# Other order at the stage borders of a Strassen-style macaron block, and the mixer's weight tiles at high addresses

## The chip, the cores and the metric

The kernel runs on one core of a Trainium2 chip. The metric is the device time of one execution in microseconds (us). The engines are TensorE (PE in the profile, with its weight loads as PEld), VectorE (DVE), ScalarE (ACT) and GpSimd (POOL); SyncE (SP) issues most transfers. Each engine works through its own queue in a fixed order and waits at an instruction until what it needs is there.

## The reference

One layer on x of 1024 tokens by 1024 channels, all in float32:

```
x = x + 0.5 * SwiGLU_1(RMSNorm(x))          # FFN 1: gate, up 1024x2816, down 2816x1024
h = RMSNorm(x); p = h @ W_in                # u, v of the gating; q, k, v, z, b, a of the delta rule
x = x + concat(A, B) @ W_out                # A: chunked spatial gating, B: gated delta rule, 4 heads of 128
x = x + 0.5 * SwiGLU_2(RMSNorm(x))          # FFN 2, the same sizes
y = RMSNorm(x)
```

`swiglu(x) = (silu(x @ w_gate) * (x @ w_up)) @ w_down`. In B the short convolution, SiLU and an L2 norm are put on the queries and keys, and a decay matrix `exp(g_i - g_j)` per head and chunk is made from the a column group of the projection.

## The kernel before

**Products.** Each float32 operand is split into a high and a low part (`split`, L60 to L62: ACT casts the high part, DVE subtracts it to get the low part), and `mm3` (L53) makes three matmuls of one product: high by high, high by low, low by high. The FFNs are computed with seven products instead of eight. `Combos` (L107) holds the transposed, normed x as quarters B11, B12, B21, B22 and as four combinations T1 to T4 of them. For 128 tokens at a time, `blocks` transposes (L95, TensorE with an identity) two token tiles, and writes the quarters and the combinations with `put` (ACT L118 high part, then DVE or POOL L119 low part).

**FFN.** `ffn` (L173) loads the gate and up weights of 22 column blocks (`load_gu`, L189, tiles `graw`, POOL makes the combinations `s` at L199, and the split tiles are `ga` and `gs`). Block 0 is done with plain products (`gu_plain`, L237) in two halves of 256 columns each, so that it can begin when half of x is normed; blocks 1 to 21 use the seven products (`gu`, L257), which need all of B and T. `start1` (L475) and `start2` (L625) hold the order of this beginning: norms of x (ACT square, DVE scale at L82 or L502), `blocks`, the two `gu_plain`. Between blocks, sums of weights and hidden values are stored for the down products. The down stage (L367 to L444) works through 7 rows of a plan (k = 0 to 6) with 6 units each, a unit being a left and a right tile that are loaded (`prepare`, L377, three units ahead), split (tile `unit`) and multiplied.

**FFN 1 to mixer.** While the last rows of the down stage run, each finished token tile is normed and transposed into `hT` (`to_mid`, L518). `z0` (L528) is a filler handed to `ffn`: its weights (`zraw`, split to `wz`) are loaded first, and it then makes 8 token tiles' first half of z and of the b and a columns. It allocates in the pools of FFN 1 (`sf`, `graw`). `middle` (L684) follows: the a columns become `xa` (L745 to L762), a matmul with `csa` (L763 to L766) sums them along the chunk, the result goes out and comes back broadcast as `grb`, and `decay` (L780) makes the decay matrices E from that (DVE L791 to L796, ACT exponentials). `v0` is the first half of the values, 8 token tiles of 24 matmuls; `keys` (L879) makes the keys of a head with the convolution (`pad`, `acc`, L863 to L869) and their transposes (`kst`, L838).

**Mixer to FFN 2.** The last of the mixer are the u1 products (mm<-wk at L53). Then 16 groups of transposes bring the mixer's output into `yT` (ACT and DVE `actT`), and `w_out` (L577) multiplies by W_out, whose weight tiles `wo` are split in the `gsp` ring of FFN 2.

**What sets the order.** The program is written as Python generators. A list scheduler of the tile framework puts each engine's queue in order from the order in which the code is written and from when tiles come free. Tiles live in pools; the pools of a stage are laid one behind the other in SBUF in the order in which they are opened, and those of the next stage lie over them, so a new tile waits for the old tile at its address. Opened at L555 to L561 are the mixer's pools: in the program before, its weight tiles `wk` (pool `wp`) lie at byte 114112 to 146880 of a partition, over FFN 1's `graw` and `sf` and what lies next to them, and FFN 2's `wo` tiles at 181184 to 209856 lie over the key tiles `kst` and their neighbours..

## Time and profile before

| | before |
|---|---|
| median of 3 runs (lowest to highest) | 1855.46 us (1854.37 to 1859.35) |
| profiled execution: time / span in the profile | 1855.36 us / 1853.6 us |
| mean granted TensorE clock | 0.988 |
| busy: PE, DVE, ACT, POOL | 96%, 63%, 37%, 40% |

In the rows of a timeline, the columns are start, busy time, engine, line, operation, out<-in, tile size, how many are put together, and in brackets the idle time of that engine just before and who released it. A table of windows gives for each stretch the engines' busy time with their number of instructions, and then PEclk, the granted clock (1.00 is full).

### The profile page before, as it was taken

Reading aid. Unit: us, or ns where it says so; the run is one execution under the profiler, and the core shown is the slowest. Engines: PE = TensorE matmul, PEld = TensorE weight load, DVE = VectorE, ACT = ScalarE, POOL = GpSimd, SP = SyncE. Lnnn points to the kernel's source line nnn. Section 1 sums busy time; section 2 is a strip of 40 time slices with the busy share of each in tenths; the row PEclk is TensorE's granted clock in tenths of the full one; section 3 lists DMA queues with packets and bytes.
Section 4 is the critical chain, followed back from the end, with each engine's and each line's share of the span. In section 5 each row is a group of like instructions: output and inputs, shape, how many; then the busy total and the mean of one; then the engine's idle time right before and its main releaser. Section 6 shows DMA issues by size and latency. Waiting matters only on the chain.

```text
span 1853.6 us, 25526 instructions
## 1 busy us (share of the span) xinstructions
PE 1788.0 (96%) x9735; PEld 1529.8 (83%) x9735; DVE 1175.8 (63%) x1529; ACT 685.8 (37%) x1193; POOL 746.7 (40%) x585
## 2 busy tenths in 40 slices
PE   5999999998999998998999999989999999999997
PEld 4888888887788888998788999978888888878886
DVE  6867776554565474668755344587676776656546
ACT  5433333322443353432344542443333323244433
POOL 5567576564140012121032420366576665614001
PEclk8999999999999998999999999999999999999999
DMA  5254444534957444454432354334544445495744
GB/s 206 102 171 140 165 139 150 185 138 168 337 190 261 135 168 138 139 178 131 145 87 71 92 199 138 114 97 148 176 148 161 152 141 177 152 337 193 263 144 148
DMA packets 134732, 302.27 MB, mean 163 GB/s; under 512 B 27441, under 2 KB 42065, under 8 KB 134609
## 3 DMA queue, kind: packets, MB, share of 16 engines
q1 hardware_dynamic: 132112, 296.20, 47.2%
q10 hardware_dynamic: 2496, 4.44, 0.7%
q8 instruction: 76, 1.25, 0.3%
q14 instruction: 48, 0.39, 0.1%
HBM read 208.83 MB, written 91.77 MB: 162 GB/s over the span
## 4 chain that ended last, share of the span: by engine, by line
PE 82%; DVE 6%; DMA 4%; POOL 3%; issue 2%; ACT 1%; SPq 0%; POOLq 0%; DVEq 0%; ACTq 0%
PE mm L53 46%; PE ax L53 33%; PE ax L95 1%; POOL s L199 1%; PE sd L53 1%; DMA graw<-in_f2gu_dram 1%; POOL rs L70 1%; DVE acc L867 1%; POOL t L286 1%; PE sc L53 1%; DMA left<-hq 1%; DVE E L791 0%; POOL s L286 0%; DVE unit L62 0%; DVE o L82 0%
## 5 line engine op out<-in xcount | busy, mean ns | idle before, releaser
L53 PE MATMUL mm<-unit 128*128 128x512 f32 x1056 | 243.1, 390 | 5.7 <-ACT unit L61 3.9
L199 POOL TENSOR_TENSOR s<-graw 128x512 f32<-128x512 f32 x84 | 129.2, 1538 | 273.8 <-DMA graw<-in_f2gu_dram 128.5
L53 PEld LDWEIGHTS mm<-unit 128*128 128x128 f32 x1056 | 197.6, 188 | 48.3 <-ACT unit L61 4.7
L62 DVE TENSOR_TENSOR ga<-graw,ga 128x512 fp32r<-128x512 f32 x134 | 152.0, 1136 | 108.6 <-ACT ga L61 107.9
L61 ACT CAST gs<-s 128x512 fp32r<-128x512 f32 x168 | 104.1, 622 | 297.6 <-PE ax L53 144.6
L62 DVE TENSOR_TENSOR unit<-left,unit 128x1024 fp32r<-128x1024 f32 x84 | 101.8, 1215 | 137.2 <-ACT unit L61 137.2
L53 PE MATMUL ax<-T,gs 128*128 128x512 f32 x792 | 183.1, 389 | 0.0
L53 PE MATMUL ax<-unit 128*128 128x512 f32 x792 | 180.5, 389 | 0.0
L53 PEld LDWEIGHTS ax<-T,gs 128*128 128x128 f32 x792 | 148.7, 188 | 30.9
L53 PEld LDWEIGHTS ax<-unit 128*128 128x128 f32 x792 | 148.7, 188 | 30.9
L62 DVE TENSOR_TENSOR gs<-s,gs 128x512 fp32r<-128x512 f32 x168 | 169.3, 1009 | 2.5 <-ACT gs L61 0.3
L61 ACT CAST unit<-left 128x1024 fp32r<-128x1024 f32 x84 | 82.5, 982 | 235.9 <-PE ax L53 101.8
L53 PE MATMUL mm<-B,ga 128*128 128x512 f32 (+1 forms) x864 | 167.1, 348 | 0.2 <-DVE ga L62 0.2
L53 PE MATMUL mm<-T,gs 128*128 128x512 f32 x720 | 166.4, 389 | 0.0
L53 PEld LDWEIGHTS mm<-T,gs 128*128 128x128 f32 x720 | 135.1, 188 | 28.1
L53 PEld LDWEIGHTS mm<-B,ga 128*128 128x128 f32 x864 | 140.3, 195 | 19.2 <-DVE ga L62 0.4
L53 PE MATMUL mm<-actT,wk 128*128 128x512 f32 x576 | 150.2, 402 | 0.0
L70 POOL TENSOR_TENSOR rs<-rs,half 128x1 f32<-128x1 f32 (+1 forms) x29 | 20.2, 697 | 317.5 <-DVE rs L76 317.4
L53 PE MATMUL mm<-wk,actT 128*128 128x256 f32 x960 | 126.5, 289 | 2.3 <-ACT wk L61 1.8
L53 PE MATMUL ax<-B,ga 128*128 128x512 f32 x528 | 127.1, 390 | 0.0
L53 PEld LDWEIGHTS mm<-wk,actT 128*128 128x128 f32 x960 | 120.2, 195 | 3.5 <-ACT wk L61 2.1
L53 PEld LDWEIGHTS mm<-actT,wk 128*128 128x128 f32 x576 | 103.5, 188 | 19.1 <-ACT ev L736 0.2
(239 smaller groups left out, 3044.4 us busy)
## 6 DMA issues: line engine op xcount, KB each, us to landing
left<-hq SPq DMA_DIRECT2D x70, 512.0 KB, 5.0
graw<-in_f1gu_dram SPq DMA_DIRECT2D x44, 512.0 KB, 5.5
wq<-t SPq DMA_DIRECT2D x44, 512.0 KB, 2.8
hq<-s SPq DMA_DIRECT2D x44, 512.0 KB, 3.2
graw<-in_f2gu_dram SPq DMA_DIRECT2D x44, 512.0 KB, 5.0
right<-wq SPq DMA_DIRECT2D x40, 512.0 KB, 4.9
wd<-in_f1wd_dram SPq DMA_DIRECT2D x22, 512.0 KB, 6.6
hq<-sg SPq DMA_DIRECT2D x22, 512.0 KB, 3.7
```

What stands on the lines that cost most here:

```text
L53: nc.tensor.matmul(*args, **kw)
L61: nc.scalar.copy(h, src)
L62: nc.vector.tensor_tensor(l, src, h, op=ALU.subtract)
L70: nc.gpsimd.tensor_tensor(o, i, half[:, :w], op=ALU.pow)
L95: nc.tensor.transpose(ps[:, i * P:(i + 1) * P], blk(i), ident)
L199: nc.gpsimd.tensor_tensor(f, u, v, op=op)
L286: nc.gpsimd.tensor_tensor(o, u, v, op=op)
L867: nc.vector.scalar_tensor_tensor(acc, pad[:, j:j + 512], cw[:, blk, j:j + 1], acc, op0=ALU.mult, op1=ALU.add)
```

## The change

The order at the borders between the stages is written differently, and some tiles move. No arithmetic is changed.

- **Beginning of the FFNs.** `put_sums` takes the splits of T1 to T4 out of `blocks`; all of them come after the second `gu_plain`. The norms of the second half of x are written ahead of the first `gu_plain`. The sums of the second half are held in the x pool. x is loaded in the order 0, 4, 1, 5 and 2, 6, 3, 7, the second four earlier.
- **Down stage.** `prepare` loads the right tile first.
- **z.** The weights are loaded as two tiles of 1088 columns in the ring `post`, which the down stage's right tiles use too, and z's products go to the banks "mm" instead of "ax".
- **Mixer.** The pools are opened in another order: `wk` now lies at byte 176576 to 211392, above all others, and its tiles have 2176 columns. The weights of v0 are loaded ahead of the rest of `middle`, and three of v0's token tiles come before the sum along the chunk.

```diff
...
 
-        def sums(self):
-            return [self.qp.tile([P, 2, 512], F32, tag="post", name="f", bufs=4) for _ in range(2)]
-
-
-        def blocks(self, i, pp, xns, uv, b12=None, late=False, eng=nc.gpsimd):
+        def sums(self, p=None):
+            if p is None:
+                return [self.qp.tile([P, 2, 512], F32, tag="post", name="f", bufs=4) for _ in range(2)]
+            return [p.tile([P, 2, 512], F32, tag="x", name="f") for _ in range(2)]
+
+
+        def blocks(self, i, pp, xns, uv, b12=None):
             def tr(j, q):
...
             nc.vector.tensor_tensor(t2, b22p, t1, op=ALU.subtract)
+            self.put("B22", i, b22p, nc.vector)
             nc.vector.tensor_tensor(t4, b21p, t2, op=ALU.subtract)
-            self.put("B22", i, b22p, nc.vector)
-            yield
-            if not late:
-                self.put("T2", i, t2, nc.vector)
+            yield
+
+        def put_sums(self, i, names, engs):
+            t3, t1, t2, t4 = self.f[i]
+            for n, eng in zip(names, engs):
+                if n == "T3":
+                    nc.gpsimd.tensor_tensor(t3, t2, t3, op=ALU.subtract)
+                self.put(n, i, {"T1": t1, "T2": t2, "T3": t3, "T4": t4}[n], eng)
                 yield
-            self.put("T1", i, t1, nc.gpsimd)
-            yield
-            nc.gpsimd.tensor_tensor(t3, t2, t3, op=ALU.subtract)
-            self.put("T3", i, t3, eng)
-            yield
-            if not late:
-                self.put("T4", i, t4, eng)
-                yield
-
-        def late(self, i):
-            _, _, t2, t4 = self.f[i]
-            self.put("T2", i, t2, nc.vector)
-            yield
-            self.put("T4", i, t4, nc.gpsimd)
-            yield
 
...
             left, right = gtile(F32, "left"), post("right")
-            nc.sync.dma_start(left[:, :n], hq[u][:, l, :n])
             if isinstance(r, tuple):
...
                 nc.sync.dma_start(right[:, :n], wq[u][:, r, :n])
+            nc.sync.dma_start(left[:, :n], hq[u][:, l, :n])
             t = bp.tile([P, 2, 2, 2, 512], F32R, tag="cmb", name="unit", bufs=3)
...
     nc.scalar.dma_start(ident, a["cst"][:, 0:P])
-    xs = load_x(xdram, (0, 1))
+    xs = load_x(xdram, (0, 4))
     g = grow("ffn1_norm")
-    xs.update(load_x(xdram, (4, 5)))
+    xs.update(load_x(xdram, (1, 5)))
 
...
             next(weights)
+            xs.update(load_x(xdram, (2, 6, 3, 7)))
             b = b12()
...
             together(*parts, n=2)
-            together(*parts, weights, n=2)
-            xs.update(load_x(xdram, (2, 3, 6, 7)))
-            f.gu_plain(slice(0, 256), b)
+            together(*parts, weights)
             rest = xi(2) + xi(3)
...
                 nc.vector.scalar_tensor_tensor(x, x, rs[:, i:i + 1], g, op0=ALU.mult, op1=ALU.mult)
-            together(*parts)
+            f.gu_plain(slice(0, 256), b)
             b = b12()
-            parts = [cb.blocks(i, f.X, xi(i), cb.sums(), b, eng=nc.vector) for i in range(2, 4)]
-            together(*parts, n=4)
+            for i in range(2, 4):
+                together(cb.blocks(i, f.X, xi(i), cb.sums(xp), b))
             f.gu_plain(slice(256, 512), b)
-            together(*parts)
+            V, G = nc.vector, nc.gpsimd
+            together(*(cb.put_sums(i, ("T2", "T1", "T3", "T4"), (V, G, V, G)) for i in range(4)))
 
...
             for i in range(4):
-                r = rp.tile([P, 544], F32, tag="sf", name="zraw", bufs=4)
-                nc.sync.dma_start(r, a["wz0"][i // 2][:, i % 2 * 544:i % 2 * 544 + 544])
+                if i % 2 == 0:
+                    raw = qp.tile([P, 1088], F32, tag="post", name="zraw", bufs=4)
+                    nc.sync.dma_start(raw, a["wz0"][i // 2])
+                r = raw[:, i % 2 * 544:i % 2 * 544 + 544]
                 w = rp.tile([P, 2, 544], F32R, tag="graw", name="wz", bufs=4)
...
             for t in range(8):
-                o = bank(ps[1], "ax")
+                o = bank(ps[0], "mm")
                 h = st["hT"][t // 4]
...
         ps_a, ps_s, ps_m = psums(mid, (2, 1, 3))
-        wp = pool(mid, "wp")
+        tl = pool(mid, "tl")
+        up = pool(mid, "up")
+        lv = pool(mid, "lv")
         ep = pool(mid, "ep")
         ts = pool(mid, "ts")
-        up = pool(mid, "up")
-        tl = pool(mid, "tl")
-        lv = pool(mid, "lv")
         kp = pool(mid, "kp")
+        wp = pool(mid, "wp")
         yblk = middle(tc, nc, a, locals())
...
                 normed(x, g2, x, junk)
-            together(cb.blocks(i, pp, xi, uv, b, late=True))
+            together(cb.blocks(i, pp, xi, uv, b))
+            together(cb.put_sums(i, ("T1", "T3"), (nc.gpsimd, nc.gpsimd)))
         together(second)
...
             together(f.load_gu(0, True))
-            f.gu_plain(slice(0, 256), b)
             xns = {}
...
                     normed(xs[i + 4 * j], g2, xns[i][j])
+            f.gu_plain(slice(0, 256), b)
             c = b12()
-            parts = [cb.blocks(2, pp, xns[2], cb.sums(), c)]
-            together(*parts, n=4)
-            together(cb.late(0), cb.late(1))
-            parts.append(cb.blocks(3, pp, xns[3], cb.sums(), c))
-            together(parts[1], n=4)
+            for i in range(2, 4):
+                together(cb.blocks(i, pp, xns[i], cb.sums(xp), c))
             f.gu_plain(slice(256, 512), c)
-            together(*parts)
+            V, G = nc.vector, nc.gpsimd
+            together(*(cb.put_sums(i, ("T2", "T4"), (V, G)) for i in range(2)),
+                     *(cb.put_sums(i, ("T2", "T1", "T3", "T4"), (V, G, V, G)) for i in range(2, 4)))
 
...
 
-    def load_w(src):
+
+    def load_w(src, off=0):
         raw = wp.tile([P, src.shape[-1]], F32, tag="raw", name="raw", bufs=2)
         nc.sync.dma_start(raw, src)
-        s = wp.tile([P, 2, src.shape[-1]], F32R, tag="wk", name="wk", bufs=4)
+        s = wp.tile([P, 2176], F32R, tag="wk", name="wk", bufs=4)[:, off:off + 2048].rearrange("p (s n) -> p s n", s=2)
         split(s[:, 0], s[:, 1], raw)
...
 
-    def token_steps(srcs, n, evac, act, tiles=range(8), part=KC):
-        ws = [load_w(s).rearrange("p s (k n) -> p s k n", k=4) for s in srcs]
+    def token_steps(srcs, n, evac, act, tiles=range(8), part=KC, ahead=False):
+        ws = [load_w(s, 16).rearrange("p s (k n) -> p s k n", k=4) for s in srcs]
+        if ahead:
+            yield
         for t in tiles:
...
         return f
+
+    def steps(name, ch, ev, **kw):
+        w = a[f"w{name}"][ch]
+        return token_steps([w[0], w[1]], 256, ev, hT, **kw)
+
+
+    v0 = steps("v", 0, spill("v", 0, nc.scalar.copy), ahead=True)
+    next(v0)
 
...
     nc.vector.tensor_tensor(hv(xa), hv(xa), alog.unsqueeze(2).to_broadcast([P, HEADS, 8]), op=ALU.mult)
+    together(islice(v0, 3))
     psg = bank(ps_a, "ax")
...
 
-    def steps(name, ch, ev, **kw):
-        w = a[f"w{name}"][ch]
-        return token_steps([w[0], w[1]], 256, ev, hT, **kw)
-
-    v0 = steps("v", 0, spill("v", 0, nc.scalar.copy))
     for h in range(HEADS):
```

**Where the queues change.** On TensorE at the end of FFN 1, where `wz` are z's weights, `xa` and `csa` the sum along the chunk, `wk` the mixer's weights (here v0's, then the first key's) and `actT` the normed x; before:

```order
L95 MATMUL ax<-ident,xn 128x128 x8
L53 MATMUL ax<-wz,actT 128x264 x144
L53 MATMUL ax<-xa,csa 128x32 x3
L771 MATMUL ax<-ident,gc 32x128
L53 MATMUL mm<-wk,actT 128x256 x192
L53 MATMUL mm<-actT,wk 128x512 x48
```

and now:

```order
L95 MATMUL ax<-ident,xn 128x128 x8
L53 MATMUL mm<-wz,actT 128x264 x144
L53 MATMUL mm<-wk,actT 128x256 x72
L53 MATMUL ax<-xa,csa 128x32 x3
L53 MATMUL mm<-wk,actT 128x256 x4
L777 MATMUL ax<-ident,gc 32x128
L53 MATMUL mm<-wk,actT 128x256 x116
L53 MATMUL mm<-actT,wk 128x512 x48
```

72 of the 192 matmuls of v0 have moved ahead of the sum along the chunk, and 4 ahead of the transpose of its result; z's products go to "mm".

On ScalarE, behind the last evictions (`ev`) of u1, where `actT` is the mixer's transposed output and `wo` a weight tile of W_out; before:

```order
L61 CAST wo<-graw 128x512 x3
L1129 ACTIVATE ev<-mm 128x256
L61 CAST wo<-graw 128x512 x3
L1129 ACTIVATE ev<-mm 128x256
L61 CAST wo<-graw 128x512
L1129 ACTIVATE ev<-mm 128x256 x4
L102 CAST actT<-ax 128x4x128 x16
L61 CAST wo<-graw 128x512 x15
```

and now:

```order
L1135 ACTIVATE ev<-mm 128x256 x8
L102 CAST actT<-ax 128x4x128 x5
L61 CAST wo<-graw 128x512
L102 CAST actT<-ax 128x4x128 x2
L61 CAST wo<-graw 128x512
L102 CAST actT<-ax 128x4x128 x3
L61 CAST wo<-graw 128x512
L102 CAST actT<-ax 128x4x128 x3
L61 CAST wo<-graw 128x512
L102 CAST actT<-ax 128x4x128 x3
L61 CAST wo<-graw 128x512 x18
```

Seven casts of `wo` that stood among the evictions of u1 now stand among and behind the casts of `actT`. On VectorE at the same place, the low parts; before:

```order
L874 TENSOR_SCALAR ro<-sso 128x4
L62 TENSOR_TENSOR wo<-graw,wo 128x512 x7
L103 TENSOR_TENSOR actT<-ax,actT 128x4x128 x16
L62 TENSOR_TENSOR wo<-graw,wo 128x512 x3
L599 TENSOR_TENSOR x<-x,mm 128x256 x4
```

and now:

```order
L880 TENSOR_SCALAR ro<-sso 128x4
L103 TENSOR_TENSOR actT<-ax,actT 128x4x128 x16
L62 TENSOR_TENSOR wo<-graw,wo 128x512 x8
L593 TENSOR_TENSOR x<-x,mm 128x256 x2
L62 TENSOR_TENSOR wo<-graw,wo 128x512
L593 TENSOR_TENSOR x<-x,mm 128x256 x2
```

All low parts of `wo` now stand behind the 16 of `actT`; TensorE has 4 of the `wo` products among the transposes, where it had 17.

On TensorE between the two `gu_plain` of FFN 2, where `xn` is normed x, `ga` the split weights of block 0 and the B of the last rows is B11; before:

```order
L53 MATMUL mm<-B_10274,ga_10707 128x256 x12
L53 MATMUL mm<-B_10274,ga_10710 128x256 x12
L95 MATMUL ax<-ident,xn 128x128 x32
L53 MATMUL mm<-B_10246,ga_10701 128x256 x12
L53 MATMUL mm<-B_10246,ga_10704 128x256 x12
```

and now:

```order
L53 MATMUL mm<-B_10269,ga_10703 128x256 x12
L53 MATMUL mm<-B_10269,ga_10706 128x256 x12
L95 MATMUL ax<-ident,xn 128x128 x24
L53 MATMUL mm<-B_10242,ga_10697 128x256
L53 MATMUL mm<-B_10242,ga_10700 128x256
L95 MATMUL ax<-ident,xn 128x128 x8
L53 MATMUL mm<-B_10242,ga_10697 128x256 x11
L53 MATMUL mm<-B_10242,ga_10700 128x256 x11
```

Two of the second half's matmuls have moved ahead of the last 8 transposes. The norms of the second half, which VectorE did between the two `gu_plain`, now stand among the last additions of `w_out`, ahead of the first.

More of the change, by code (lines that the diff above doesn't have):

```diff
@@ L1042, in middle @@
     S_h = {}
-    ones = sc("ones", 16)[:, 0:1]
+    ones = sc("ones", 128)[:, 0:1]
     nc.vector.memset(ones, 1.0)
```

## The prediction

> **What bounds the kernel now.** I read the page first.
>
> ```profile
> span 1853.6 us, 25526 instructions
> PE 1788.0 (96%) x9735; PEld 1529.8 (83%) x9735; DVE 1175.8 (63%) x1529; ACT 685.8 (37%) x1193; POOL 746.7 (40%) x585
> ```
>
> TensorE is busy 1788.0 of 1853.6 us, and the change leaves its matmuls in number and size as they are. So only two things can move the time: the 65.6 us in which TensorE stands, and the stretches in which its clock is low. The view of TensorE's waits adds the first up by cause:
>
> ```profile
> PE mm L53 <- DVE up L274: 5.1, 1, 5.1
> PE ax L53 <- DVE xa L762: 4.9, 1, 4.9
> ```
>
> The two longest single ones behind the kernel's first instructions are these (us in total, times, longest): at z's weights and at the mixer's beginning, which the change writes anew. For the clock I read the table of windows, and TensorE's timeline for a shorter wait just ahead of the last of them:
>
> ```profile
> 438.00:456.00 18.00, 12.86 (x46) 10.05 (x45) 10.78 (x13) 6.37 (x11) 4.71 (x4) 0.81 0.62 208
> 724.00:740.00 16.00, 15.13 (x102) 14.84 (x103) 14.20 (x12) 6.26 (x11) 8.83 (x6) 0.78 0.59 175
> 855.00:860.00 5.00, 5.00 (x42) 4.96 (x43) 4.58 (x11) 2.27 (x5) 0.00 (x0) 1.00 0.45 157
> ...
> 854.89 2.02 PE L53 MATMUL ax<-vm,u 128*128 128x128 f32 x16 [2.63 <-DVE vm L1078]
> ```
>
> The number before the last two is the granted clock: 0.81 and 0.78 behind the waits of 5.1 and 4.9 us, and full behind one of 2.63. A long wait costs its length and then slow matmuls. The sum below goes against the profiled execution's 1855.36 us, of which 1.8 lie outside the span; the median of the runs, 1855.46, is practically the same.
>
> **1. z's weights leave block 20: −7.8.** The timelines of TensorE, SyncE and ScalarE there, and of TensorE at the same place in FFN 2:
>
> ```profile
> 445.42 5.49 PE L53 MATMUL mm<-T,ga 128*128 128x512 f32 x12 [5.14 <-DVE up L274]
> ...
> 438.11 8.21 SPq L532 DMA_DIRECT2D zraw<-in_wz_dram  x4
> ...
> 443.36 0.65 ACT L61 CAST wz<-zraw 128x544 fp32r<-128x544 f32 x1 [10.52 <-DMA zraw<-in_wz_dram]
> ...
> 1605.74 2.88 PE L53 MATMUL mm<-B,gs 128*128 128x512 f32 x12
> ```
>
> The cast of `wz` stands in ScalarE's queue ahead of the work of block 20 and waits 10.52 us for its load; VectorE's low part waits for the cast, `up` behind it, and TensorE 5.14 us for `up`. Its next 12 matmuls take 5.49 us, where 12 take 2.88 warm. In the changed program neither load nor cast is in this block: 5.14 + 2.61 = 7.75 us go. What is late next is nothing that I see: FFN 2 has no z and runs through this place without a wait.
>
> In the down stage the loads and eight splits (four on ScalarE at 0.65, four on VectorE) come again, in rows 4 and 5 of the plan. A unit keeps TensorE for 24 matmuls, two groups like the last row, 5.4 us after overlap. The cover is that units are loaded up to three ahead; a load takes
>
> ```profile
> left<-hq SPq DMA_DIRECT2D x70, 512.0 KB, 5.0
> ```
>
> 5.0 us from issue to landing, while two units ahead are 10.9. With two of the four `post` tiles held by z the lead falls to one or two units. I take 0; if the cover is gone it costs what the first rival says. The right tile loaded ahead of the left one, and the banks "mm" for z, cost nothing by themselves: both halves are needed by the same unit, and the bank of the first tile is free before z begins.
>
> **2. Start of FFN 1: −1.0.** VectorE's group of the second half's norms, POOL at that time, TensorE at the second `gu_plain`, and the same scale in FFN 2:
>
> ```profile
> L502 DVE SCALAR_TENSOR_TENSOR x<-x,rs,grow 128x1024 f32<-128x1024 f32 x4 | 8.4, 2120 | 3.5 <-POOL rs L70 3.5
> ...
> 33.67 7.89 POOL L119 TENSOR_TENSOR T<-f,T 128x512 fp32r<-128x512 f32 x4
> ...
> 48.27 5.25 PE L53 MATMUL mm<-B,ga 128*128 128x256 f32 x29
> ...
> ...
> 1207.67 1.28 DVE L82 SCALAR_TENSOR_TENSOR xn<-x,rs,grow 128x1024 f32<-128x1024 f32 x1
> ```
>
> The four scales take 2.12 us each, beside POOL's low parts of T; elsewhere 1.28. Now POOL has only two of these ahead of its next wait, so about two scales get fast (−1.7). All splits of T leave the path between the norms and the second products. Against that, tile 4 is squared second, but POOL's power for the second half still stands behind four `s` combinations, and the two `blocks` run one behind the other. I put the resumption at 48.27 some 1.5 us earlier and the beginning 0.5 later. The row for it is missing, so −3 to +2.
>
> **3. FFN 1 to mixer: −4.6.** The timeline of TensorE:
>
> ```profile
> 693.71 0.66 PE L95 MATMUL ax<-ident,xn 128*128 128x128 f32 x4 [2.07 <-DVE actT L103]
> 698.12 17.68 PE L53 MATMUL ax<-wz,actT 128*128 128x264 f32 x144
> 720.67 1.44 PE L53 MATMUL ax<-xa,csa 128*128 128x32 f32 x6 [4.87 <-DVE xa L762]
> 724.61 1.01 PE L53 MATMUL mm<-wk,actT 128*128 128x256 f32 x3 [1.83 <-ACT wk L61]
> 725.88 22.29 PE L53 MATMUL mm<-wk,actT 128*128 128x256 f32 x165 [0.26 <-DVE wk L62]
> 751.53 11.18 PE L53 MATMUL mm<-actT,wk 128*128 128x512 f32 x48
> 762.54 5.91 PE L53 MATMUL mm<-wk,actT 128*128 128x256 f32 x48
> 769.73 0.66 PE L838 MATMUL ax<-ident,kst 128*128 128x128 f32 x4
> 771.03 4.13 PE L53 MATMUL mm<-actT,wk 128*128 128x512 f32 x17
> ```
>
> The wait of 2.07 is for a bank "ax" which z's product holds; in "mm" it doesn't. z ends at 715.8, v0 at 751.5. In these 35.7 us TensorE needs 1.8 for the sum and its transpose and 192 × 0.123 (5.91 / 48) = 23.6 for v0 warm; 10.3 are waits and slow clock. All could go: −12.4 at most.
>
> But VectorE sets the next date:
>
> ```profile
> 728.12 1.82 DVE L791 TENSOR_TENSOR E<-grb,gc 128x512 f32<-128x512 f32 x1 [1.17 <-DMA grb<-grd]
> ...
> 749.87 0.68 DVE L794 TENSOR_TENSOR E<-E,gc 128x512 f32<-128x512 f32 x1
> ...
> 758.48 2.46 DVE L62 TENSOR_TENSOR wk<-raw,wk 128x1024 fp32r<-128x1024 f32 x2 [5.66 <-ACT wk L61]
> ...
> 761.37 2.33 DVE L867 SCALAR_TENSOR_TENSOR acc<-pad,cw,acc 128x512 f32<-128x512 f32 x3
> 764.94 0.49 DVE L865 TENSOR_SCALAR acc<-pad,cw 128x512 f32<-128x512 f32 x1 [1.25 <-ACT pad L863]
> ...
> 768.27 0.74 DVE L867 SCALAR_TENSOR_TENSOR acc<-pad,cw,acc 128x512 f32<-128x512 f32 x1
> ```
>
> The E chain runs from 728.12, 7.45 us behind the sum, to 750.55 without a hole. In the time of before, less 2.07: z ends at 713.7, 72 matmuls of v0 at 722.6, the sum follows, E starts at 730.1 and ends at 752.5, 2 us later than now, though TensorE is through v0 at 739.1, the first key's 48 at 750.1 and the next 48 at 756.0. Behind E, VectorE still has two `wk` (2.46), and the first `acc` (0.49 + 2.33): 757.8, SiLU and the way to TensorE 0.7 (769.73 less 769.01, the end of the last `acc`), so the first `kst` at 758.5, a wait of 2.5. The second `pad` copy stands behind that SiLU on ScalarE (0.65, as the cast of `wz`); the second `acc` takes 764.94 to 769.01, or 4.07, then 0.7: second `kst` at 763.9, a wait of some 4. The next key's products start 1.3 later, less 0.23 for the one matmul moved ahead: 765.0 instead of 771.03, −6.1. A wait of 4 us lies between 2.6, which left the clock at 1.00, and the two of about 5, one of which cost 2.61 in slow matmuls; I add 1.5. So −4.6, between −12.4 (VectorE has nothing late) and −2.
>
> [...]
>
> **4. Mixer to w_out: +6.2.** TensorE, ScalarE and VectorE:
>
> ```profile
> 1092.37 0.60 PE L95 MATMUL ax<-ident,ya 128*128 128x128 f32 x4
> ...
> 1101.58 55.79 PE L53 MATMUL mm<-wo,actT 128*128 128x256 f32 x463
> ...
> 1093.00 9.44 ACT L102 CAST actT<-ax 128x512 fp32r<-128x512 f32 x16
> ...
> 1078.76 5.48 DVE L62 TENSOR_TENSOR wo<-graw,wo 128x512 fp32r<-128x512 f32 x7 [6.15 <-ACT wo L61]
> ```
>
> Now the first `wo` are split while u1 runs, hidden behind its matmuls, and w_out begins at 1101.58. In the changed program `wo` lies on the weights of u1 and its splits stand behind. ScalarE then has 16 × 0.59 + 4 × 0.65 (the cast of `wz`) = 12.0 us from 1093.0, to 1105.0; VectorE's last `actT` is 0.6 later (9.44 / 16), its first `wo` low part another 0.6: 1106.2. That is 4.6 later, and the 13 matmuls that no longer run among the transposes come on top, 13 × 0.1205 (55.79 / 463) = 1.6. Ends: +3.5 if ScalarE's casts of `wo` fit into its waits for TensorE, +9 if the pause lowers the clock.
>
> **5. Start of FFN 2: −4.4.**
>
> ```profile
> 1207.07 0.60 PE L95 MATMUL ax<-ident,xn 128*128 128x128 f32 x4
> 1218.29 12.23 PE L53 MATMUL mm<-B,ga 128*128 128x256 f32 x96
> ...
> 1210.95 0.68 DVE L119 TENSOR_TENSOR B<-ax,B 128x512 fp32r<-128x512 f32 x1
> ...
> 1216.55 0.68 DVE L119 TENSOR_TENSOR B<-ax,B 128x512 fp32r<-128x512 f32 x1
> ```
>
> The second half's products wait 11.2 us for 32 transposes, whose norms are made in that time. These now stand among the last additions of w_out, which leave VectorE idle, so the transposes can start at 1207.1 and the first B at 1208.2. From the first B to B11 of the last token tile VectorE took 1210.95 to 1217.2, with one scale of 1.28 in it that goes: 5.0. That gives 1213.2, and 1.0 for the last 8 transposes: 1214.2. With the two matmuls moved ahead (0.24) it is −4.3, and −0.1 for the clock; ends −5.5 and −2.5.
>
> **Sum.** −7.8 − 1.0 − 4.6 + 6.2 − 4.4 = −11.6, so 1855.36 − 11.6 = 1843.8 us.
>
> **Rivals.** *z's weights stall the down stage (the other side).* If the ring `post` has lost its lead, each unit of rows 4 and 5 takes 5.0 (load) plus a cast and a low part of 1.2 each (2.46 / 2, `wk` in part 3, a tile of that size) instead of 5.4, 2.0 more; 12 units are 24 us, or 1868. From six units on it is slower than before, by over 0.3% from nine on. For it: both kinds of tile share four buffers. Against it: z's tiles are split soon after they land, so two or three units at most should feel it.
> *The mixer's gain comes whole.* VectorE runs E faster, since fewer splits stand beside it, and no `kst` is late: −12.4 in part 3, so 1843.8 − 7.8 = 1836.
> *The gain is given back.* w_out pays +9 and the first two keys wait until nothing of part 3 is left, so only −7.8 − 1.0 − 4.4 + 9 = −4.2 stays: 1851. VectorE without a hole for 22 us speaks for it.
>
> **How the numbers follow.** The forecast has 0.60, the whole gain 0.14, the gain given back 0.18, the stall 0.08. The bounds of parts 2 to 5 are independent; about ±6 covers them, so the forecast alone is 1838 to 1850. To leave out no more than 2 in 10 I reach to 1833 and 1853. A measurement of this kernel tells about 0.3% (5.6 us) from no change: the stall is slower, the given-back case the same but for a little, and a little of the forecast is the same: faster 0.78, same 0.15, slower 0.07.
>
> **What would show it.** Right: no wait behind `up` in block 20; no wait between z and v0's first 72 matmuls; waits of 2 to 4 us at the first two `kst`; w_out's long run beginning 13 to 14 us behind u1's end instead of 9.2; the second `gu_plain` of FFN 2 beginning 7 us behind the first instead of 11. Wrong: waits for `unit` in rows 4 and 5, an E chain that starts later than 17 us behind z's end, or a `gu` that waits for T, whose splits now come last.

## The result, and the profile after

| | before | after | ratio, 95% interval |
|---|---|---|---|
| median, us | 1855.76 (1854.37 to 1859.35, 4 runs) | 1842.04 (1841.22 to 1842.99, 4 runs) | 0.9923, 0.9906 to 0.9940 |
| the same pair on another chip | 1859.15 (1855.65 to 1873.39, 24 runs) | 1849.05 (1842.96 to 1864.33, 10 runs) | 0.9947, 0.9916 to 0.9978 |
| profiled execution / its span | 1855.36 / 1853.6 | 1841.22 / 1839.4 | |

The changed kernel is faster by 13.7 us (0.8%); in the second measurement, made last, by 10.1 (0.5%). Neither interval contains 1. The profile after is of an execution of 1841.22 us. Its page begins:

```profile
span 1839.4 us, 25484 instructions
PE 1784.1 (97%) x9735; PEld 1524.8 (83%) x9735; DVE 1191.7 (65%) x1531; ACT 686.6 (37%) x1193; POOL 747.9 (41%) x583
```

TensorE is busy 3.9 us less for the same 9735 matmuls (less slow clock: 0.992 in the mean, 0.988 before), so it stands 10.3 us less. VectorE is busy 15.9 us more, with only two instructions more: on the whole its instructions got slower (1191.7 / 1531 = 0.778 us in the mean, 1175.8 / 1529 = 0.769 before).

The timelines of TensorE can be laid over each other, since the order of its work is nearly the same. Each row below is the stretch from one event to the next, and the rows add up to the difference of the spans (−0.2 is left over behind the last):

| stretch, us | before | after | difference | forecast |
|---|---|---|---|---|
| start to block 1's second product (T, `gs`), FFN 1 | 64.76 | 65.08 | +0.3 | −1.0 |
| to the first unit of the down stage | 407.32 | 399.25 | −8.1 | −7.8 |
| first row of the plan | 31.09 | 32.69 | +1.6 | 0 |
| rows 2 to 6, to z's first matmul | 184.88 | 184.92 | 0 | 0 |
| to the second key's products | 82.98 | 74.88 | −8.1 | −4.6 |
| to u1's end | 321.34 | 320.36 | −1.0 | 0 |
| to w_out's end | 103.18 | 107.86 | +4.7 | +6.2 |
| to block 1's second product, FFN 2 | 37.56 | 35.81 | −1.8 | −4.4 |
| to the first unit of FFN 2 | 399.21 | 397.51 | −1.7 | 0 |

First block 20 of FFN 1, in TensorE's timeline of after (start, length, engine and line, matmuls; in brackets a wait and who ended it):

```profile
440.44 2.88 PE L53 MATMUL mm<-T,ga 128*128 128x512 f32 x12
```

The wait of 5.14 for `up` is gone, and the 12 matmuls take 2.88 instead of 5.49. From z's end on, the same timeline reads:

```profile
689.51 17.69 PE L53 MATMUL mm<-wz,actT 128*128 128x264 f32 x144
707.04 8.64 PE L53 MATMUL mm<-wk,actT 128*128 128x256 f32 x72
715.52 0.75 PE L53 MATMUL ax<-xa,csa 128*128 128x32 f32 x6
716.67 13.91 PE L53 MATMUL mm<-wk,actT 128*128 128x256 f32 x116
...
745.78 5.92 PE L53 MATMUL mm<-wk,actT 128*128 128x256 f32 x35 [2.75 <-DVE wk L62]
751.54 0.60 PE L844 MATMUL ax<-ident,kst 128*128 128x128 f32 x4
...
755.52 0.66 PE L844 MATMUL ax<-ident,kst 128*128 128x128 f32 x4 [2.25 <-ACT kst L875]
...
756.82 10.93 PE L53 MATMUL mm<-actT,wk 128*128 128x512 f32 x47
```

The waits of 2.07, 4.87 and 1.83 are gone, v0 runs at full speed behind z (8.64 / 72 = 0.12 each, at a clock of 1.00), and at the first key two new waits stand, 2.75 and 2.25. The 35 matmuls behind the first of them take 0.17 each (5.92 / 35) instead of 0.12: the granted clock is 0.50 from 746.78 to 750.19. VectorE's timeline gives the cause of the waits:

```profile
722.22 0.69 DVE L797 TENSOR_TENSOR E<-grb,gc 128x512 f32<-128x512 f32 x1 [4.98 <-DMA grb<-grd]
...
743.91 0.68 DVE L800 TENSOR_TENSOR E<-E,gc 128x512 f32<-128x512 f32 x1
```

The E chain lasts 744.59 − 722.22 = 22.4 us, as before, and everything behind it is late by it. Between mixer and FFN 2 TensorE's timeline reads:

```profile
1077.18 0.60 PE L95 MATMUL ax<-ident,ya 128*128 128x128 f32 x4
...
1089.49 57.38 PE L53 MATMUL mm<-wo,actT 128*128 128x256 f32 x476 [2.52 <-DVE wo L62]
...
1187.53 2.90 PE L53 MATMUL mm<-B,ga 128*128 128x256 f32 x22 [0.66 <-DVE ga L62]
...
1197.88 1.91 PE L95 MATMUL ax<-ident,xn 128*128 128x128 f32 x16
...
1206.08 12.18 PE L53 MATMUL mm<-B,ga 128*128 128x256 f32 x94
```

w_out's long run starts 12.3 us behind u1's end (9.2 before) and has 13 matmuls more in it; the second half's products of FFN 2 start 8.2 us behind the first transposes instead of 11.2.

### The profile page after: what moved, and what is told of

The parts are those of the page before. It is cut to its first block, busy times and chain, and to the rows that moved or that the text cites. A ratio compares the mean times of both kernels' runs of the same rounds, so it can differ in the third digit from the quotient of the medians.

```text
span 1839.4 us, 25484 instructions
## 1 busy us (share of the span) xinstructions
PE 1784.1 (97%) x9735; PEld 1524.8 (83%) x9735; DVE 1191.7 (65%) x1531; ACT 686.6 (37%) x1193; POOL 747.9 (41%) x583
## 4 chain that ended last, share of the span: by engine, by line
PE 78%; DVE 8%; DMA 5%; POOL 4%; issue 3%; ACT 2%; SPq 0%; POOLq 0%; DVEq 0%; ACTq 0%
PE mm L53 43%; PE ax L53 32%; POOL s L191 1%; POOL t L278 1%; DMA left<-hq 1%; DVE acc L873 1%; PE ax L95 1%; PE sd L53 1%; DMA graw<-in_f1gu_dram 1%; POOL s L278 1%; PE sc L53 1%; DVE T L119 0%; DVE unit L62 0%; DVE wk L62 0%; DVE E L797 0%
## 5 line engine op out<-in xcount | busy, mean ns | idle before, releaser
L62 DVE TENSOR_TENSOR ga<-graw,ga 128x512 fp32r<-128x512 f32 x134 | 155.9, 1166 | 99.9 <-ACT ga L61 99.2
L53 PE MATMUL ax<-T,gs 128*128 128x512 f32 x792 | 183.1, 389 | 0.0
```

The costliest lines, as they stand in the source:

```text
L53: nc.tensor.matmul(*args, **kw)
L62: nc.vector.tensor_tensor(l, src, h, op=ALU.subtract)
```

## Experiments

Kernels e1 to e8 were run once each, with a profile; e9 to e12 together on one chip, timed beside the kernel before. Times of single runs scatter by several us (1842.96 to 1864.33 in the ten of e9) for a reason found in the last part, so verdicts on single runs go by stretches. The four stretches that matter, in us, are measured between the same events as in the table above; the times in this table are those of the profiled executions:

| kernel | time | z to second key | u1 to w_out's end | w_out's end to block 1, FFN 2 | first row of plan |
|---|---|---|---|---|---|
| before | 1855.36 | 82.98 | 103.18 | 37.56 | 31.09 |
| after | 1841.22 | 74.88 | 107.86 | 35.81 | 32.69 |
| e1 z's old tiles | 1857.15 | 78.20 | 107.84 | 35.86 | 32.68 |
| e2 mixer's old pools | 1837.82 | 80.13 | 103.17 | 35.15 | 31.13 |
| e3 v0 two steps ahead | 1851.55 | 77.22 | 110.47 | 34.76 | 31.09 |
| e4 FFN 2's pools | 1846.74 | 78.04 | 104.36 | 35.99 | 31.11 |
| e5 e4 and E's fourth head | 1840.16 | 72.13 | 104.35 | 34.79 | 32.68 |
| e6 e3 and E's fourth head | 1851.04 | 73.80 | 109.30 | 35.76 | 31.07 |
| e7 weight sums later | 1850.90 | 78.28 | 109.37 | 35.99 | 31.10 |
| e8 norms behind products, FFN 2 | 1856.03 | 77.71 | 109.36 | 37.82 | 32.71 |
| e9 after again | 1858.78 | 77.68 | 110.42 | 36.20 | 33.90 |
| e10 E's fourth head | 1851.78 | 71.87 | 110.44 | 36.13 | 33.98 |
| e11 mixer's old pools | 1845.54 | 79.88 | 103.17 | 34.74 | 33.97 |
| e12 e4, e5 and e7 together | 1840.59 | 71.93 | 104.35 | 35.83 | 32.57 |

### z's tiles (e1)

```diff
-                if i % 2 == 0:
-                    raw = qp.tile([P, 1088], F32, tag="post", name="zraw", bufs=4)
-                    nc.sync.dma_start(raw, a["wz0"][i // 2])
-                r = raw[:, i % 2 * 544:i % 2 * 544 + 544]
+                r = rp.tile([P, 544], F32, tag="sf", name="zraw", bufs=4)
+                nc.sync.dma_start(r, a["wz0"][i // 2][:, i % 2 * 544:i % 2 * 544 + 544])
```

> The changed kernel with one part undone: z's weights are again four tiles of the ring sf, whose loads and splits stand among block 20 of FFN 1; z's products stay in the banks mm. Theory (ScalarE's cast waits for the load, and block 20 behind it): TensorE waits about 5 us in block 20 again and its next matmuls are slow by 2.6, so 7.9 us more, about 1850. Rival (the two big tiles in the ring post cost something in the down stage, such as the slow first row of the plan, 1.5 us): that comes back as a gain, and it is 6.3 more, about 1848.5.

TensorE's timeline of e1 in block 20:

```profile
445.23 4.61 PE L53 MATMUL mm<-T,ga 128*128 128x512 f32 x12 [4.68 <-DVE up L266]
```

The wait and the slow matmuls are back, 4.68 + (4.61 − 2.88) = 6.4 us, and 0.47 more in a longer wait for the first unit. From block 1's second product to the first unit it takes 406.43 instead of 399.25: +7.2. So the tiles alone carry 7.2 of the 8.1 us. The first row of the plan stays at 32.7: its 1.6 us do not come from z's move, and the rival theory falls.

### Who pays for the new order of the mixer's pools (e2, e4)

e2 puts the mixer's seven pools back in the old order; e4 leaves them and reorders FFN 2's instead.

```diff
-        tl = pool(mid, "tl")
-        up = pool(mid, "up")
-        lv = pool(mid, "lv")
+        wp = pool(mid, "wp")
         ep = pool(mid, "ep")
         ts = pool(mid, "ts")
+        up = pool(mid, "up")
+        tl = pool(mid, "tl")
+        lv = pool(mid, "lv")
         kp = pool(mid, "kp")
-        wp = pool(mid, "wp")
```

> The changed kernel with the mixer's pools opened in the old order, so that wk lies low again, over z's own tiles. Theory (the address is what lets v0 run ahead, and what holds back wo): v0's weights wait for z's end again, TensorE stands between z and v0, and of the 8.3 us won at this border only the 2.5 from z's banks stay, 5.8 more; w_out begins 9.2 us behind u1 again instead of 12.3, 4.7 less; together +1, about 1843. Rival (w_out's late beginning has another cause than the address): no part of it comes back, +6, about 1848.

```diff
-        bp = pool(f2, "bp")
         rp = pool(f2, "rp")
-        gp = pool(f2, "gp")
         qp = pool(f2, "qp")
+        gp = pool(f2, "gp")
+        bp = pool(f2, "bp")
```

> The changed kernel with FFN 2's pools opened in another order (rp, qp, gp, bp), so that wo no longer lies over the weights of u1; two wo tiles are then split ahead of the transposes, and 19 of w_out's matmuls stand among them. Theory (w_out waits for wo's low part, which stands behind 16 of actT): w_out's wait of 2.5 us goes and its long run is 15 matmuls shorter, so 4 to 4.7 us less, about 1837.5. Rival (the transposes and their splits are the bound, and wo is ready in time anyway): under 1 us, about 1841.5.

TensorE's timeline of e2 at both places:

```profile
709.09 1.49 PE L53 MATMUL ax<-xa,csa 128*128 128x32 f32 x6 [4.87 <-DVE xa L767]
...
1088.78 55.79 PE L53 MATMUL mm<-wo,actT 128*128 128x256 f32 x463
```

The wait of 4.87 is back to the hundredth and the border at z costs 5.3 more; w_out is cheaper by 4.7. One edit does both, so terms 3 and 4 are two sides of where the mixer's weights lie. That w_out needn't pay shows in e4: with FFN 2's tiles laid so that `wo` doesn't fall on the weights of u1, u1 to w_out's end takes 104.36 with the mixer's new pools kept, 3.5 of the 4.7 back. Nor is 4.7 what w_out usually pays. The wait of 2.52 for `wo` is the same in all eight profiles with the new order of the mixer's pools and the old one of FFN 2's, but only in after and e1 does the clock stay full behind it (1.00 in after from 1089.49 to 1146.90; the stretch takes 107.86 there and 107.84 in e1). In the other six (e3, e6 to e10) it drops (to 0.50 in e3 from 1096 to 1100), and the stretch takes 109.3 to 110.5, 6.1 to 7.3 more than before; in e9:

```profile
1101.16 59.93 PE L53 MATMUL mm<-wo,actT 128*128 128x256 f32 x476 [2.52 <-DVE wo L62]
```

The same 476 matmuls took 57.38 in after. What e4 won there it lost elsewhere, at a place that it doesn't touch, the subject of the next part.

### The fourth head's E on GpSimd (e3, e5, e6)

e3 draws two steps of v0 ahead of the sum, not three, to start the E chain sooner:

```diff
-    together(islice(v0, 3))
+    together(islice(v0, 2))
```

> The changed kernel with two instead of three of v0's token tiles ahead of the sum along the chunk. Theory (VectorE's E chain, which follows the sum, sets when the first kst are ready): xa is ready at 712.6 us, just when two tiles are done, so the sum, E and both kst come 2.9 us earlier, the waits of 2.75 and 2.25 us shrink to 2 together, and the time falls by about 2.9 to 1839. Rival (TensorE's own work sets it, the waits only fill its slack, or xa comes later than the two tiles): no gain, or a new wait at the sum, 1842 to 1843.

The sum came 2.8 us earlier, but the second key's products 2.3 later. In e4 they were 3.2 later with the mixer's code as in after. GpSimd, VectorE, ScalarE and TensorE of e4, one fence each:

```profile
734.50 9.12 POOL L799 TENSOR_TENSOR E<-csa,grb 128x512 f32<-128x512 f32 x1 [3.94 <-DMA grb<-grd]
```

```profile
735.85 0.68 DVE L799 TENSOR_TENSOR E<-csa,grb 128x512 f32<-128x512 f32 x1
...
741.27 1.21 DVE L62 TENSOR_TENSOR wk<-raw,wk 128x1024 fp32r<-128x1024 f32 x1
```

```profile
744.77 0.63 ACT L801 ACTIVATE E<-E 128x512 f32<-128x512 f32 x1 [5.82 <-POOL E L800]
```

```profile
746.96 4.62 PE L53 MATMUL mm<-wk,actT 128*128 128x256 f32 x24 [2.87 <-ACT pad L869]
...
756.83 0.66 PE L844 MATMUL ax<-ident,kst 128*128 128x128 f32 x4 [3.53 <-ACT kst L875]
```

And the same instruction of GpSimd in after:

```profile
735.64 1.53 POOL L799 TENSOR_TENSOR E<-csa,grb 128x512 f32<-128x512 f32 x1 [3.79 <-DMA grb<-grd]
```

The same instruction takes 1.53 in one execution and 9.12 in another. In e4 it comes up while VectorE runs a stream of operations, nearly all of 0.68 us, without a hole until 742.48; it ends 1.1 us behind the stream. ScalarE, in order, waits 5.82 for its exponential, the copies of `pad` stand behind that, and TensorE waits 2.87 and 3.53 for them. It took 8.65 to 9.12 in six of the seven profiles with this code (e1, e3, e4, e7, e8, e9) and 1.53 only in after's first; in before, e2 and e11, with the old pools, 1.34 to 1.67. In after it comes up amid the same stream and gets in. It begins 0.31 us behind the start of one of VectorE's operations there, and 0.35 to 0.57 us behind in the six others; seven cases don't show whether that decides it. So the changed kernel's first profile was the lucky one, and usually the border costs some 3 us more (77.68 to 78.28 in e1, e4 and e7 to e9, 74.88 in after). The trace of e4 shows GpSimd's operation held up and not slowed in proportion: some 13 operations of VectorE pass before it ends. By what means it is held up the traces don't show; in e4 and e9 it ended 1.1 us behind VectorE's stream.

e5 and e6 give that operation of the fourth head to VectorE, on top of e4 and of e3:

```diff
-            eng = nc.vector if hf else nc.gpsimd
+            eng = nc.vector if hf or h == 3 else nc.gpsimd
```

> The kernel of e4 (FFN 2's pools in another order), with GpSimd's part of the fourth head's E on VectorE. In e4 GpSimd's operation for that head took 9.1 us while VectorE ran without a pause, ScalarE waited 5.8 us for it, and the first pad copy behind it came late. Theory (the GpSimd operation is shut out while VectorE streams, and that alone is what e4 lost): both waits for pad and kst shrink from 6.4 us to 4 or less, with no slow clock behind them, so 4 to 6 us less than e4's 1846.7, 1841 to 1842.5, and 1 to 2 us more if TensorE's clock drops elsewhere. Rival (the 9.1 us are only what the profile shows, and ScalarE or the address of wo made the loss): no change, 1846.

> The kernel of e3 (two of v0's tiles ahead of the sum), with the same part of E on VectorE, so that GpSimd can't be shut out there. Theory (VectorE's E chain sets the first kst): measured from z's end, the sum comes 2.9 us earlier than in the changed kernel, or 1 to 2.9 if xa is not ready, E ends by as much earlier less the 1.3 us that VectorE takes over, and the second key's products start 0 to 1.6 us earlier. Rival (TensorE's own work is the bound): they start at the same distance from z's end, 56.6 us from the end of the 192 products of z, or later.

TensorE's timeline of e5, then of e6:

```profile
746.29 5.92 PE L53 MATMUL mm<-wk,actT 128*128 128x256 f32 x35 [2.71 <-DVE wk L62]
752.05 0.60 PE L844 MATMUL ax<-ident,kst 128*128 128x128 f32 x4
...
753.38 0.60 PE L844 MATMUL ax<-ident,kst 128*128 128x128 f32 x4
```

```profile
749.29 0.66 PE L844 MATMUL ax<-ident,kst 128*128 128x128 f32 x4 [0.17 <-ACT kst L875]
...
754.60 0.66 PE L844 MATMUL ax<-ident,kst 128*128 128x128 f32 x4 [3.76 <-ACT kst L875]
```

In e5 the waits for `pad` and `kst` are gone and the border takes 72.13, 5.9 less than e4: the blocked operation was the cause. The wait for `wk`, behind the E chain, stays at 2.71, and the 35 matmuls behind it are slow (5.92), which the expectation had excluded. In e6 the first `kst` comes 67.0 us behind z's first matmul, 2.3 sooner than in e10 (69.3), so the chain's beginning does move it; but a `wk` and a copy stand among the second `acc` in e6 and behind it in e10, the second `kst` waits 3.76, and the border is 1.9 longer than e10's 71.87. Half of the expectation held.

### The start of FFN 1 (e7)

The weight sums of chunk 0 (GpSimd) go behind block 1, away from T's low parts:

```diff
-            if c % 2:
+            if c % 2 == 0:
+                hidden_sums(c // 2 - 1)
+            elif c > 1 or fill is None:
                 weight_sums(c // 2)
-            else:
-                hidden_sums(c // 2 - 1)
             gu(c, (A, X)[c % 2])
+            if c == 1 and fill is not None:
+                weight_sums(0)
```

Only FFN 1 has a filler `fill`, so FFN 2 keeps its order.

> The changed kernel with GpSimd's first sums of the down weights moved behind block 1 of FFN 1, so that GpSimd does not run them beside VectorE's seven low parts of T. Theory (VectorE's low parts of T take 1.32 us each because GpSimd works beside them, against 0.68 alone, and ga of block 1 is late for that): they take 0.7 to 1.0 us, the wait of 1.42 us in block 1 goes, and block 1 starts its second product 1 to 1.5 us earlier; the time falls by as much, if no other stretch's clock changes. Rival (they wait for the casts or run slow by themselves): no change there.

TensorE's timeline of after, and VectorE's:

```profile
60.62 0.63 PE L53 MATMUL ax<-B,ga 128*128 128x512 f32 x2
62.67 2.57 PE L53 MATMUL ax<-B,ga 128*128 128x512 f32 x10 [1.42 <-DVE ga L62]
```

```profile
51.72 9.21 DVE L119 TENSOR_TENSOR T<-f,T 128x512 fp32r<-128x512 f32 x7
60.86 1.76 DVE L62 TENSOR_TENSOR ga<-graw,ga 128x512 fp32r<-128x512 f32 x1
```

and VectorE's and TensorE's of e7:

```profile
51.95 5.92 DVE L119 TENSOR_TENSOR T<-f,T 128x512 fp32r<-128x512 f32 x7
```

```profile
60.03 2.91 PE L53 MATMUL ax<-B,ga 128*128 128x512 f32 x12
62.78 8.32 PE L53 MATMUL ax<-T,gs 128*128 128x512 f32 x36
```

In after VectorE's low parts of T, gathered behind the plain products, take 9.21 / 7 = 1.32 each beside GpSimd, block 1's `ga` comes late, and TensorE waits 1.42. With the sums moved the seven take 5.92 (0.85 each), the wait is gone, and block 1's second product starts at 62.78 instead of 65.08, of which 0.6 comes from an earlier beginning; the 1.7 left are a little more than expected. The kernel's time hides that: GpSimd's E took 9.02 in this run, and the clock was lower at other places (0.989 in the mean, 0.992 in after).

### Norms ahead of the plain products in FFN 2 (e8)

```diff
             together(f.load_gu(0, True))
+            f.gu_plain(slice(0, 256), b)
             xns = {}
...
-            f.gu_plain(slice(0, 256), b)
             c = b12()
```

> The changed kernel with the norms of the second half of FFN 2's beginning written behind the first plain products again, all else as changed. Theory (the norms ahead win less than forecast because they hold up ga and because SiLU's table load and two sg stand ahead of the first B): from the end of w_out's last products to block 1's T the changed kernel takes 1.75 us less than before; this one takes 1.5 to 2.5 us more than the changed one, though its first plain products start without the waits of 0.66 and 0.15 us. Rival (the 1.75 us come from the splits of T, which this keeps behind the second products): no difference.

TensorE's timeline of e8:

```profile
1194.44 11.68 PE L53 MATMUL mm<-B,ga 128*128 128x256 f32 x96
...
1214.75 2.79 PE L95 MATMUL ax<-ident,xn 128*128 128x128 f32 x12 [3.51 <-DVE f L150]
```

From w_out's end to block 1's second product it takes 37.82 instead of 35.81: the move of the norms is worth 2.0 us. It is made up of two things: without the move the first half's 96 matmuls run through without a wait (11.52 from the end of w_out; 12.84 in after, with waits of 0.66 and 0.15 for `ga`), and what follows takes 26.30 instead of 22.97. So 3.3 are won and 1.3 given back.

### The kernel again, and the parts together (e9 to e12)

e9 is after unchanged; e10 has the fourth head's E of e5 alone; e11 is e2 again; e12 has e4, e5 and e7 together.

> The changed kernel itself, unaltered, on another chip and day, to see what of it is steady. In its first profile GpSimd's operation for the fourth head's E took 1.5 us; in five experiments with the same mixer code it took about 9, and some waits of 2 to 3 us were followed by slow matmuls and others not. Theory (both depend on the phase in which an execution comes there): its runs scatter over 1841 to 1848, and the profile may show the 9 us. Rival (the phase is fixed by the program, and the experiments shifted it): all runs lie at 1841 to 1843 again and the profile shows 1.5 us.

> The changed kernel with GpSimd's part of the fourth head's E on VectorE, nothing else. Theory (that operation is shut out by VectorE's stream in most executions, and sets the first pad copy): the second key's products start 2 to 6 us earlier, counted from z's first, than in the changed kernel on the same chip, and the median is 2 to 5 us below that of the changed kernel run beside it. Rival (VectorE, which now has two operations more, is the bound): it is the same or 1.3 us slower.

> The kernel of e2 (mixer's pools in the old order, all else changed) timed. In its one look it took 1837.8 us, 4 less than the changed kernel: from z's first product to the second key it takes 5.2 us more, from u1's end to the end of w_out 4.7 less, and 4.5 less lay in stretches with the same instructions and another clock. Theory (moving wk up is worth nothing on the sum): its median lies within 2 us of the changed kernel's beside it. Rival (it is really 4 us faster): its median is 3 to 5 us below.

> The changed kernel with three edits: FFN 2's pools in another order (e4), the fourth head's E on VectorE (e5), and the first sums of the down weights behind block 1 (e7). Theory (each takes away a wait that it showed by itself: 3.5 us at w_out, 2 to 5 at the first keys, 1.7 in block 1): the median is 5 to 9 us below the changed kernel beside it, 1834 to 1838. Rival (what is won at one border is lost again at the next through waits and slow clock): 1840 or more.

| kernel, all on one chip | median, us (lowest to highest, runs) | ratio to before, 95% interval |
|---|---|---|
| before | 1859.15 (1855.65 to 1873.39, 24) | |
| e9 after again | 1849.05 (1842.96 to 1864.33, 10) | 0.9947, 0.9916 to 0.9978 |
| e10 E's fourth head | 1845.17 (1840.25 to 1853.16, 9) | 0.9912, 0.9882 to 0.9942 |
| e11 mixer's old pools | 1846.94 (1843.48 to 1857.49, 10) | 0.9922, 0.9892 to 0.9953 |
| e12 all three | 1839.15 (1834.42 to 1843.03, 4) | 0.9874, 0.9820 to 0.9929 |

e9 scatters more than was expected, and so did before, up to 1873. GpSimd's E was blocked in e9's profile (9.03). e10 lies 3.9 below e9, within what was expected, though the intervals overlap; in the profiles its second key's products start 5.8 us earlier, counted from z's first (71.87 against 77.68). e11 lies 2.1 below e9, between the 2 of its theory and the 3 of its rival, with intervals that overlap: the two are not told apart, and the 4 us of e2's single run are not confirmed. So the new pools of the mixer, taken as they are, win nothing that this can show: what they save at z they pay at w_out and through GpSimd. The two stretches together took 183.3 and 183.1 us with the old pools and all else changed (e2, e11), 186.0 to 188.1 with the new ones (e1, e7, e8, e9) and 182.7 in after alone; before, they took 186.2. e12 has the lowest median, 9.9 below e9 beside it, from four runs. That is more than the 5 to 9 expected, and its interval overlaps e9's a little and e10's more. The absolute time expected of it was missed by 1.2 us, as all kernels of this measurement lay higher. TensorE's waits of e12, from the list by cause:

```profile
PE mm L53 <- ACT unit L61: 4.3, 2, 2.3
...
PE mm L53 <- DVE wk L62: 2.6, 1, 2.6
```

The waits for `wo`, `kst`, `pad` and block 1's `ga` aren't there; the E chain's 2.6 is.

**Where the scatter comes from.** From the second key's products to u1's end, after and e9 run the same program with the same waits to a few tenths. The table of windows for that stretch, after and e9 (the number before the last two is the granted clock):

```profile
756.82:1077.18 320.36, 312.53 (x2443) 275.39 (x2442) 185.46 (x411) 117.94 (x298) 87.38 (x127) 1.00 0.37 116
```

```profile
761.26:1088.85 327.59, 319.76 (x2443) 281.18 (x2441) 185.52 (x411) 117.82 (x298) 87.44 (x127) 0.97 0.37 114
```

The stretch takes 7.2 us longer in e9, all of it in matmuls at a lower clock. The first row of the plan shows the same: TensorE stands for the first unit in every kernel, and the row takes 31.1 us in six profiles (waits of 0.73 to 2.23), 32.6 to 32.7 in five (1.97 to 2.55) and 33.9 to 34.0 in three (2.02 to 2.21). Waits of the same length cost nothing, 1.6 or 2.9 us.

The clock's record shows most of the difference. In each of the 14 profiles the granted clock is 1.00 or 0.50 for whole steps of a grid of 3.41 us. Windows cut along that grid at the first row, for e9 and then before (the second number is the time in which TensorE is busy, the one before the last two the clock):

```profile
461.89:465.30 3.41, 1.21 (x5) 0.44 (x3) 0.71 (x2) 1.04 (x1) 0.00 (x0) 1.00 1.05 407
465.30:468.71 3.41, 2.65 (x7) 2.15 (x7) 2.94 (x4) 1.58 (x2) 0.31 (x1) 0.50 0.97 344
468.72:472.12 3.40, 3.40 (x9) 2.64 (x8) 1.80 (x3) 1.05 (x1) 3.40 (x3) 0.50 0.87 290
```

```profile
468.17:471.58 3.41, 1.99 (x9) 1.31 (x7) 1.06 (x2) 0.59 (x1) 0.00 (x0) 1.00 1.04 405
471.59:475.00 3.41, 2.16 (x8) 1.58 (x9) 2.87 (x3) 2.02 (x3) 0.00 (x0) 1.00 1.00 377
```

In e9 the wait falls into one step, TensorE is busy for 1.21 of its 3.41 us, and the next two steps run at half clock. In before a wait nearly as long (1.92 against 2.21) is divided between two steps, 1.99 and 2.16 us busy, and the clock stays full. Between 60 and 1800 us the 14 profiles have 50 steps at full clock in which TensorE was busy under 0.44 of the time (1.50 of 3.41 us), and each was followed by half clock. In after the step from 743.37, busy for 1.00 us, was followed by 0.50, and the one from 753.61, busy for 1.50, by 1.00. Of 36 steps from 0.44 to 0.55, 15 were (after's first row is one, at 1.81 of 3.41 us), and of all steps above 0.55, 4. One step at half clock costs up to 1.7 us (half of 3.41) and two cost up to 3.4, hence the 1.6 and the 2.9. The grid lies differently against the program in each profile (the first unit starts 0.49 us into a step in before, 0.86 in after, 2.92 in e9), so whether a wait of about 2 us falls into one step or is divided between two is chance. This is read from the traces; no run moved the grid by intent.

The mean clock of the profiled execution was 0.992 in after and 0.984 in e9: by an estimate from these two, some 15 of the 17.6 us between them are clock.

## Why the prediction was right, point by point

The time on record, 1843.8, lies 1.8 above the first measurement and 5.3 below the second, and both lie within the range. The large stages behave as the forecast said. That the first number is met within 2 us is partly luck: single terms were off by up to 3.5, both ways, and cancel.

1. **Block 20 (−7.8):** right, −8.1, and e1 gives 7.2 of it back by undoing z's tiles alone. The down stage shows no lost lead: rows 2 to 6 of the plan take 184.92 instead of 184.88. The rival of the other side, the stall through the ring `post`, is refuted.
2. **Start of FFN 1 (−1.0):** +0.3. The four scales got faster as forecast (6.88 us together instead of 8.40), but the resumption at 48.27, forecast 1.5 earlier, came at 48.31. Block 1 begins 1.4 earlier (60.62 instead of 62.01), with 8 transposes moved ahead of the resumption. The splits of T did leave the path between the norms and the second products, but the step put at nothing what they cost behind it: they came back at block 1 through VectorE and GpSimd, as a wait of 1.42 for `ga` (e7). The prediction listed a `gu` that waits for late splits as a sign of error; what was late here are the weights' splits, queued behind T's.
3. **FFN 1 to mixer (−4.6):** the mechanism held, E chain first, `kst` behind it. The size was off by 3.5. The 1.5 for a slow clock was in the wrong place: the clock dropped behind the first wait, and the 35 matmuls there took 5.92 instead of 35 × 0.123 = 4.3, 1.6 more. The second `kst` waits for VectorE's second `acc`, which runs from 750.74 to 754.81 without a hole, so the slow matmuls only shortened the wait there, to 2.25 instead of some 4. Of the other 2.0, the sum came 1.0 earlier behind z's first matmul than forecast (33.6 instead of 34.5), E started 6.7 behind the sum and not 7.5, and from E's end to the end of the first `acc` it took 4.9 instead of 5.3. The first wait stood at `wk`, one place ahead of `kst`. In after no wait came near 4 us, but six experiments have one of 3.0 to 3.8 at the second `kst` (e1, e3, e4, e6, e7, e8), and a step at half clock followed each, which cost 1.6 to 1.7 us in the matmuls there: the prediction's 1.5 was right in size. What the prediction did not have at all is the block on GpSimd, which usually takes some 3 of the 8 back; with it the term would have been about right by luck.
4. **Mixer to w_out (+6.2):** right in kind (e2: 4.7 by the pools alone), 1.5 too large in this profile. In the six profiles in which the clock drops behind the wait it takes 6.1 to 7.3, toward the +9 that the forecast gave for that case, so in those the 6.2 is about met or passed, for a reason that it had left out of its sum. ScalarE's copies with the casts of `wo` between them, and VectorE's first low parts behind, in after:

```profile
1077.81 2.65 ACT L102 CAST actT<-ax 128x512 fp32r<-128x512 f32 x5
...
1086.29 1.60 ACT L102 CAST actT<-ax 128x512 fp32r<-128x512 f32 x3
```

```profile
1088.76 4.89 DVE L62 TENSOR_TENSOR wo<-graw,wo 128x512 fp32r<-128x512 f32 x8
```

   The forecast gave ScalarE 12.0 us for 16 copies and four casts, by the pace of the copies in before (0.59). They took 1087.89 − 1077.81 = 10.1, and VectorE's first `wo` comes 0.9 behind them instead of 0.6. So the long run began 12.3 behind u1's end and not 13.8, short of the 13 to 14 named as a sign.
5. **Start of FFN 2 (−4.4):** the step that failed is the first B, put 1.1 behind the start of the transposes (1208.2 behind 1207.1). It took 1200.55 − 1197.88 = 2.7, as ScalarE's and VectorE's timelines show:

```profile
1197.47 1.28 ACT L243 ACT_TABLE_LOAD   x1 [4.73 <-DVE xn L82]
```

```profile
1199.19 0.75 DVE L244 TENSOR_TENSOR sg<-sg,mm 128x256 f32<-128x256 f32 x2 [2.19 <-ACT sg L243]
1200.55 0.68 DVE L119 TENSOR_TENSOR B<-ax,B 128x512 fp32r<-128x512 f32 x1
```

   ScalarE's table load and the first SiLU now stand ahead of the B, and VectorE waits 2.19 for them; before, the load lay in the time of the first products and the SiLU among the norms. No run moved these two alone. With 1.3 lost to `ga` in the first half that is 2.9, against 2.65 missing. The rest, from the first B to the second products, was forecast at 6.0 and took 5.5.
6. **Not foreseen:** the first row of the plan (+1.6, clock) and the first unit of FFN 2 (−1.7: the wait there was 1.94 in before and 0.23 in after, in one execution each). Both are chance, and cancel: the first is a step at half clock that the wait brings in eight profiles of 14, the second a wait that differs from one execution to the next.

The rival "gain given back" (1851) is close to the second measurement's 1849, and in part for its reasons: in e9's profile w_out paid 7.2, since the clock was lower behind the pause (59.93 instead of 57.38 for the 476 matmuls), though not the 9 of the rival. Part 3 kept 5.3 of its 8.1; the first two keys did not eat up all of it. The rest of what was given back went to the blocked GpSimd and to the clock at other places. The rival "whole" (1836) did not come: E was not faster.

## What to carry to other kernels

Weights placed so that the next stage's loads don't wait (5.3 us at z, e2) were paid for here where that place is read last (4.7 at w_out), so look at both borders of a pool, and at the pools of the stage behind it: e4 got back 3.5 of the 4.7 by reordering those. When work of VectorE is gathered into a stream without holes, look at what GpSimd has to do beside it (9.12 us instead of 1.53 for one operation), and try single operations on the path on the engine that already streams (5.9 us in e5). Two profiles of one program with waits of 2 to 3 us, after and e9, lie 17.6 us apart; compare stretches with the same waits, look at the clock's record, and judge a few us by many runs.

## What the runs showed of the hardware

- GpSimd was held up beside VectorE for a whole stream: 8.65 to 9.12 us in six profiles for an operation of 1.34 to 1.67 us in four others, ended 1.1 us behind the last of some 13 operations of VectorE (e4). Where GpSimd got in, VectorE's 0.68 became 1.5 to 1.8 (after). VectorE's own chain was even 2 us shorter with GpSimd held up (20.4 in e4, 22.4 in after); the loss was that ScalarE (5.82 us in e4) and TensorE (2.87 and 3.53) stood behind GpSimd.
- The granted clock was 1.00 or 0.50 for whole steps of a grid of 3.41 us in all 14 profiles. All 50 steps at full clock in which TensorE was busy under 0.44 of the time (1.50 of 3.41 us) were followed by half clock, 15 of 36 from 0.44 to 0.55, and 4 above.
- Waits of 2.0 to 2.2 us at the same place of the program cost nothing, 1.6 or 2.9 us of slow matmuls. The clock dropped at the first row of the plan in 8 of 14 profiles, behind waits of 1.97 to 2.55 us.
- The same 2443 matmuls of the mixer ran in 320.36 us at a clock of 1.00 and in 327.59 at 0.97, with waits that differ by a few tenths.
